# Encoder trunk on one core: the HGRN2 projections of eleven (head, sequence) pairs as plain products in place of seven products of quarters

## The chip, the cores and the metric

One Trainium2 chip; the kernel runs on one of its cores. The metric is the device time of one execution in microseconds (us), the median of the runs shown.

## The reference, cut to what matters

Two sequences of 16 meta tokens and 512 tokens (528 rows, 1024 features) pass through an MLA layer with its gated MLP and a bidirectional HGRN2 layer with its gated MLP, all in float32. The change lies in the HGRN2 layer, in `h @ w_in`:

```
def hgrn2_mixer(h, w_in, lb_param, o_norm, w_o, layer_idx):
    hp = jnp.pad(h, ((0, 0), (pad, 0), (0, 0)))
    proj = hp @ w_in                        # 1024 -> 5 * 1024
    q, i, f_fw, f_bw, g = jnp.split(proj, ...)
    ...
    o_fw = gla_chunked(qh, 1.0 - ff, vh, jnp.log(ff))
    o_bw = rev(gla_chunked(rev(qh), rev(1.0 - fb), rev(vh), rev(jnp.log(fb))))
    ...
    return o.astype(h.dtype) @ w_o
```

Eight heads of 128 columns each take q, f_fw, f_bw and g (four blocks of 1024 x 128 of `w_in`) and the values i.

## The kernel before

**Number format.** A float32 operand is held as two tiles in a rounded format, a high part h and a low part l = x - h. A product of two such operands is three matmuls, h*h, h*l and l*h, into one PSUM bank. A piece of weights is a [128, 1024] tile: eight blocks of 128 rows of one 128-column output block. Features lie as `act[s]`, [128, 8, 528] in h and in l for sequence s.

**Weights.** `Weights` walks a plan, piece by piece. `get` keeps one piece split and two raw pieces loaded ahead of the one in use: `_load` issues the DMA from HBM (`wraw`, 3 buffers), `split` casts the high half on ACT (L101) and subtracts the low half on POOL or DVE (L102), into `w` (3 buffers). `on_dve` names the pieces whose low half is DVE's; the pieces "p" of the HGRN2 projections are not among them, the value pieces "v" are. A piece that the second sequence needs again is stored split to HBM when its use starts (`kept_dr<-w`, 1 MB) and read back from there for s = 1 (`w<-kept_dr`).

**Units.** `hgrn` runs 16 units (h, s), the eight heads of sequence 0 and then of sequence 1. In each, TensorE computes `project(h, s)` into four tiles z0 to z3. In eight of them it also computes `values` for two heads (96 matmuls of 256 columns, for s = 0 also 24 for the meta tokens). After each yield of a projection, `step` advances the generators: `core` of the unit before last (scores, state, output) and `gates` of the last one (activations on ACT, scans and products on DVE). A scheduler then sets each engine's order; every engine works through its own queue in that order.

**Two kinds of projection.** In the units of `PLAIN`, (0,0), (1,0), (7,0), (0,1) and (7,1), each of the four blocks is 8 x 3 matmuls of 264 columns for each half of the tokens: 192 matmuls per unit, eight banks, evacuated in turn by ACT and DVE (L958). In the eleven others `seven` computes two blocks at a time as a 2 x 2 product of quarters with seven products in place of eight: 7 x 12 matmuls for each pair, 168 per unit, 14 banks. Its inputs are sums of quarters:

- of weights: `_mix` takes two raw pieces, forms four sums on POOL (L169 to L172), and splits them as seven 512-column parts in four pieces (ACT L109, low halves on DVE and POOL L110); the four pieces are stored for s = 1 (3.5 MB for each pair, 7 MB per unit, where four plain pieces are 4 MB);
- of features: `token_sums(s)` reads x back from HBM (`y<-x_dr`), forms four sums per step on DVE (L893 to L896), and splits them into the other sequence's tiles `act[1 - s]`, in the units of `SUMS_AT`, (1,0) for s = 0 and (0,1) for s = 1.

After the products come `e1` and `e5` (ACT copies, L990 and L998), five sums from PSUM on DVE and one on POOL (L1003) for each pair. Since sequence 1's tiles hold the sums of sequence 0, `load_x1` reads sequence 1's features back at unit (7,0), eight steps in one go.

```
h, s = f[1:]
finish()
if (h, s) == (HG - 1, 0):
    load_x1()
...
gens[:] = ([core(*units[n - 2])] if n > 1 else []) + [gates(*units[n - 1])]
if (h, s) in SUMS_AT:
    gens.append(token_sums(s))
for i, _ in enumerate(project(h, s)):
    if n > 1 or i >= SKIP:
        step()
```

Of the kernel before, what the change touches and what calls it, by code (L numbers as in the profile page):

```python
# [34 lines left out]
PLAIN = ((0, 0), (1, 0), (7, 0), (0, 1), (7, 1))  # L35
SUMS_AT = ((1, 0), (0, 1))
# [37 lines left out]
class Weights:  # L74
# [82 lines left out]
    def _mix(self, key, raws):  # L157

        nc = self.nc
        i, place = key[3], key[1] == "h"  # L160
        if i == 0:
            self.sums = raws
            return self.split(raws[0], 1024, nc.vector if place else nc.vector)
        if i == 1:
            v, g = self.sums
            a11, a12, a21, a22 = v[:, :512], v[:, 512:], g[:, :512], g[:, 512:]
            s1 = self.staging()[:, :512]
            s2, s3, s4 = (a11, a21, a12) if place else (self.staging()[:, :512] for _ in range(3))
            nc.gpsimd.tensor_tensor(s1, a21, a22, op=ALU.add)  # L169
            nc.gpsimd.tensor_tensor(s3, a11, a21, op=ALU.subtract)  # L170
            nc.gpsimd.tensor_tensor(s2, s1, a11, op=ALU.subtract)
            nc.gpsimd.tensor_tensor(s4, a12, s2, op=ALU.subtract)  # L172
            self.sums = (s2, s1), (s3, s4), (a22,)
        return self.split_parts(self.sums[i - 1], nc.gpsimd if i in ((2,) if place else (2,)) else nc.vector)
# [52 lines left out]
def mixed(h, s):  # L227

    return (h, s) not in PLAIN


def piece_place(key):

    kind = key[0]
    if kind == "mix":
        return ("mix", key[2][1], key[2][3], key[3]) if key[1] == "h" else None
    if kind == "p":
        return "p", key[1], key[3]
    if kind == "v":
        return ("v", key[1], key[3]) if len(key) == 4 else ("av", key[2])  # L240
    if kind == "in":
        return "in", key[2]
    if kind in ("rope", "pair"):
        return kind, *key[2:]
    if kind in ("wo", "up"):
        return kind, key[1], key[3]
    return None
# [8 lines left out]
def weight_plan(a):  # L256
# [51 lines left out]
    for f in hgrn_order():  # L308
        if f[0] == "v":
            for p in range(2):  # L310
                add(f + (p,), a["w_hgv"][2 * f[1] + p])
        elif mixed(*f[1:]):
            for p in range(2):
                add(("mix", "h", f + (p,), 0), a["w_hg"][f[1], 2 * p], a["w_hg"][f[1], 2 * p + 1])
                for i in range(1, 4):
                    add(("mix", "h", f + (p,), i))
        else:
            for i in range(4):
                add(f + (i,), a["w_hg"][f[1], i])
# [5 lines left out]
def tile_trunk(ctx: ExitStack, tc: tile.TileContext, a: dict, dbg=None):  # L325
# [532 lines left out]
    def hgrn(e_cm):  # L858
# [9 lines left out]
        W.staging = lambda: f1.tile([128, 512], F32, tag="s1", name="s1", bufs=1)  # L868

        def part(tag):  # L870
            return f1.tile([128, HT], F32, tag=tag, name=tag)

# [9 lines left out]
        def sums(s):  # L882

            return [t.rearrange("p k (c t) -> p (k c) t", c=2) for t in act[1 - s]]

        def token_sums(s):
            th, tl = sums(s)
            for k in range(4):
                y1, y2 = staged("y1"), staged("y2")
                nc.sync.dma_start(y1, x_dr[2 + s][:, k])  # L890
                nc.sync.dma_start(y2, x_dr[2 + s][:, 4 + k])
                b11, b12, b21, b22 = y1[:, :HT], y1[:, HT:], y2[:, :HT], y2[:, HT:]
                nc.vector.tensor_tensor(b11, b12, b11, op=ALU.subtract)  # L893
                nc.vector.tensor_tensor(b12, b22, b12, op=ALU.subtract)
                nc.vector.tensor_tensor(b22, b22, b11, op=ALU.subtract)
                nc.vector.tensor_tensor(b21, b21, b22, op=ALU.subtract)  # L896
                for i, y in enumerate((y1, y2)):
                    at = slice(8 * i + k, 8 * i + k + 5, 4)
                    split(th[:, at], tl[:, at], halves(y), nc.scalar, nc.gpsimd if i == 0 else nc.vector)
                yield  # L900

# [3 lines left out]
        def load_x1():  # L905
            for k in range(NK):
                r = staged()
                nc.sync.dma_start(r, x_dr[3][:, k])
                split(act[1][0][:, k], act[1][1][:, k], r, nc.scalar, nc.vector if k % 2 else nc.gpsimd)

# [35 lines left out]
        def project(h, s):  # L946
            z = [f1.tile([128, T], F32, tag=f"z{i}", name=f"z{i}", bufs=2) for i in range(4)]
            zs[h, s] = z
            if mixed(h, s):
                for p in range(2):  # L950
                    yield from seven(h, s, p, *z[2 * p : 2 * p + 2])
                return
# [7 lines left out]

        def seven(h, s, p, za, zb):

            th, tl = sums(s)
            xh, xl = act[s]

            def get(i):
                return W.get(("mix", "h", ("p", h, s, p), i))

            def product(w, w0, block):
                wh, wl = w  # L970
                ps = bank()[:, :HT]
                for k in range(4):
                    if isinstance(block, int):
                        j = 4 * (0, 3, 1, 2)[block] + k
                        bh, bl = th[:, j], tl[:, j]
                    else:
                        k0, c0 = block
                        bh, bl = xh[:, k0 + k, c0 : c0 + HT], xl[:, k0 + k, c0 : c0 + HT]
                    ws = slice(w0 + 128 * k, w0 + 128 * k + 128)
                    mm(ps, wh[:, ws], bh, start=k == 0, stop=False)  # L980
                    mm(ps, wh[:, ws], bl, start=False, stop=False)  # L981
                    mm(ps, wl[:, ws], bh, start=False, stop=k == 3)  # L982
                return ps

            tt = nc.vector.tensor_tensor
            lo, hi = slice(0, HT), slice(HT, T)
            e1, u2, u3, e5 = (part(n) for n in ("e1", "u2", "u3", "e5"))
            w = get(0)
            p1 = product(w, 0, (0, 0))
            nc.scalar.copy(e1, p1)  # L990
            p2 = product(w, 512, (4, 0))
            tt(za[:, lo], e1, p2, op=ALU.add)
            yield
            w = get(1)
            p6 = product(w, 0, 1)
            tt(u2, e1, p6, op=ALU.add)
            p5 = product(w, 512, 0)
            nc.scalar.copy(e5, p5)  # L998
            yield
            w = get(2)  # L1000
            p7 = product(w, 0, 2)
            tt(u3, u2, p7, op=ALU.add)
            nc.gpsimd.tensor_tensor(zb[:, hi], u3, e5, op=ALU.add)  # L1003
            tt(u2, u2, e5, op=ALU.add)
            p3 = product(w, 512, (4, HT))
            tt(za[:, hi], u2, p3, op=ALU.add)
            yield
            w = get(3)
            p4 = product(w, 0, 3)
            tt(zb[:, lo], u3, p4, op=ALU.add)  # L1010
            yield
# [237 lines left out]
        if order[0][1:] in SUMS_AT:  # L1249
            gens[:] = [token_sums(0)]  # L1250
# [25 lines left out]
        for f in order[1:]:  # L1276
# [6 lines left out]
            if (h, s) == (HG - 1, 0):  # L1283
                load_x1()
# [3 lines left out]
            if (h, s) in SUMS_AT:  # L1288
                gens.append(token_sums(s))
# [549 lines left out]
```

## Time and profile before

| | us |
|---|---|
| median of 3 runs | 3004.36 (3001.76 to 3009.07) |
| the profiled execution | 3010.18 |
| its span, first to last instruction | 3008.4 |
| of it the 16 units, first projection to last | 1475.4 to 2124.9 |

The mean granted TensorE clock of the profiled execution is 0.979. In a table by stretch, a busy time next to the length of the stretch tells how much of it the engine worked, and the count of matmuls tells what that work was; PEclk is the clock that was granted, 1.00 being 2.4 GHz and 0.50 being 1.2 GHz. Matmuls overlap: each is on record for some 0.28 us and the next one starts well before its end, so what a matmul costs is the distance from start to start. A wait names the instruction whose end released the waiting one.

### The profile page before, as it was taken

How to read it: one execution, taken by the hardware profiler on the slowest of the kernel's cores; microseconds unless marked ns; L12 is line 12 of the kernel's file. 1: busy time of each engine (PE TensorE's matmuls, PEld its weight loads, DVE VectorE, ACT ScalarE, POOL GpSimd, SP SyncE). 2: the span in 40 equal slices, each digit the busy share in tenths (PEclk: the TensorE clock that was granted, in tenths of full speed). 3: DMA queues.
4: the chain of work that ended last, by engine and by line, in shares of the span. 5: the costliest groups of instructions: out<-in, count | busy, mean ns of one | idle time of the engine just before them, and what ended most of it. 6: DMA issues, size and time to landing. Idle time of an engine off the chain costs nothing.

```text
span 3008.4 us, 54907 instructions
## 1 busy us (share of the span) xinstructions
PE 2846.8 (95%) x22138; PEld 2745.2 (91%) x22138; DVE 2152.8 (72%) x2872; ACT 1376.9 (46%) x2343; POOL 1436.0 (48%) x987
## 2 busy tenths in 40 slices
PE   8889999999899999999989899999999899999997
PEld 8888899899799999999978889999999899998886
DVE  5687777857988888443477877767659888886346
ACT  3355555544543444333254565445436444444343
POOL 5344444553677776443344442101315677774333
PEclk9999999999999999999999999999999999999999
DMA  7423222366322223554556675567666222225543
GB/s 257 154 95 114 93 88 85 123 219 244 146 82 81 69 86 94 188 174 125 162 184 256 240 261 191 202 247 258 230 246 225 75 74 77 86 77 188 168 151 116
DMA packets 151758, 468.50 MB, mean 156 GB/s; under 512 B 20576, under 2 KB 29792, under 8 KB 131280
## 3 DMA queue, kind: packets, MB, share of 16 engines
q1 hardware_dynamic: 147008, 455.33, 44.9%
q10 hardware_dynamic: 3168, 5.43, 0.6%
q8 instruction: 174, 2.85, 0.4%
q0 software_dynamic: 1328, 4.23, 0.4%
q14 instruction: 80, 0.66, 0.1%
HBM read 306.23 MB, written 154.30 MB: 153 GB/s over the span
## 4 chain that ended last, share of the span: by engine, by line
PE 34%; DVE 8%; ACT 3%; DMA 2%; issue 2%; POOL 1%; SPq 0%; DVEq 0%; ACTq 0%; POOLq 0%
PE mm L1565 4%; PE mm L1563 4%; PE mm L1564 4%; PE mm L1738 2%; PE mm L1739 2%; PE mm L1737 2%; PE mm L980 2%; PE mm L982 2%; PE mm L981 2%; PE mm L420 1%; PE mm L422 1%; PE mm L421 1%; PE a L1124 1%; PE mm L921 1%; DVE w L102 1%
## 5 line engine op out<-in xcount | busy, mean ns | idle before, releaser
L420 PE MATMUL mm<-ah,w 128*128 128x264 f32 x1824 | 534.0, 293 | 28.8 <-ACT w L101 9.5
L422 PE MATMUL mm<-ah,w 128*128 128x264 f32 x1824 | 526.5, 289 | 4.5 <-DVE w L102 2.3
L421 PE MATMUL mm<-al,w 128*128 128x264 f32 x1824 | 526.0, 288 | 2.8 <-DVE al L409 2.8
L101 ACT CAST w<-wraw 128x1024 fp32r<-128x1024 f32 (+3 forms) x254 | 234.2, 924 | 348.3 <-PE mm L1739 227.0
L420 PEld LDWEIGHTS mm<-ah,w 128*128 128x128 f32 x1824 | 351.0, 192 | 34.4 <-ACT w L101 9.5
L102 POOL TENSOR_TENSOR w<-wraw,w 128x1024 fp32r<-128x1024 f32 (+3 forms) x106 | 217.7, 2054 | 311.2 <-ACT w L101 280.7
L422 PEld LDWEIGHTS mm<-ah,w 128*128 128x128 f32 x1824 | 351.2, 193 | 4.9 <-DVE w L102 2.5
L421 PEld LDWEIGHTS mm<-al,w 128*128 128x128 f32 x1824 | 351.5, 193 | 4.3 <-DVE al L409 3.9
L1563 PE MATMUL mm<-ah,w 128*128 128x264 f32 x1216 | 347.8, 286 | 8.0 <-ACT w L101 6.6
L1565 PE MATMUL mm<-ah,w 128*128 128x264 f32 x1216 | 348.1, 286 | 6.7 <-DVE w L102 6.7
L1564 PE MATMUL mm<-al,w 128*128 128x264 f32 x1216 | 346.2, 285 | 0.0
L102 DVE TENSOR_TENSOR w<-wraw,w 128x1024 fp32r<-128x1024 f32 (+2 forms) x148 | 173.2, 1172 | 224.2 <-ACT w L101 220.3
L1738 PE MATMUL mm<-gl,w 128*128 128x264 f32 (+1 forms) x1012 | 324.1, 320 | 4.3 <-DVE gl L409 4.3
L1739 PE MATMUL mm<-gh,w 128*128 128x264 f32 (+1 forms) x1012 | 322.7, 319 | 2.9 <-DVE w L102 2.0
L1737 PE MATMUL mm<-gh,w 128*128 128x264 f32 (+1 forms) x1012 | 324.4, 321 | 0.5 <-DVE acc L1749 0.5
L1563 PE MATMUL mm<-th,w 128*128 128x264 f32 x912 | 259.9, 285 | 6.9 <-ACT e L1577 5.3
L1565 PE MATMUL mm<-th,w 128*128 128x264 f32 x912 | 260.4, 286 | 0.0
L1564 PE MATMUL mm<-tl,w 128*128 128x264 f32 x912 | 260.1, 285 | 0.0
L1563 PEld LDWEIGHTS mm<-ah,w 128*128 128x128 f32 x1216 | 230.6, 190 | 8.6 <-ACT w L101 7.1
L1565 PEld LDWEIGHTS mm<-ah,w 128*128 128x128 f32 x1216 | 230.6, 190 | 7.3 <-DVE w L102 7.3
L1564 PEld LDWEIGHTS mm<-al,w 128*128 128x128 f32 x1216 | 230.8, 190 | 0.0
L1738 PEld LDWEIGHTS mm<-gl,w 128*128 128x128 f32 x1012 | 191.9, 190 | 18.3 <-DVE gl L409 4.9
(365 smaller groups left out, 8463.6 us busy)
## 6 DMA issues: line engine op xcount, KB each, us to landing
kept_dr<-w SPq DMA_DIRECT2D x79, 1024.0 KB, 6.6
w<-kept_dr SPq DMA_DIRECT2D x79, 1024.0 KB, 6.2
wraw<-w_up SPq DMA_DIRECT2D x88, 512.0 KB, 4.0
wraw<-w_dn SPq DMA_DIRECT2D x88, 384.0 KB, 3.3
g_dr<-c SPq DMA_DIRECT2D x38, 528.0 KB, 2.7
wraw<-w_hg SPq DMA_DIRECT2D x36, 512.0 KB, 4.7
wraw<-w_dn SPq DMA_DIRECT2D x25, 512.0 KB, 3.6
x_dr<-acc SPq DMA_DIRECT2D x48, 264.0 KB, 2.4
```

The source lines that it names most:

```text
L101: self.nc.scalar.copy(h[:, :n], src)
L102: engine.tensor_tensor(l[:, :n], src, h[:, :n].bitcast(F32), op=ALU.subtract)
L420: mm(out, wh[:, ws], xh[:, x0 + k, cs], start=first and i == 0, stop=False)
L421: mm(out, wh[:, ws], xl[:, x0 + k, cs], start=False, stop=False)
L422: mm(out, wl[:, ws], xh[:, x0 + k, cs], start=False, stop=last and i == n - 1)
L980: mm(ps, wh[:, ws], bh, start=k == 0, stop=False)
L1563: mm(out, wh[:, ws], bh, start=k == 0, stop=False)
L1564: mm(out, wh[:, ws], bl, start=False, stop=False)
L1565: mm(out, wl[:, ws], bh, start=False, stop=k == 3)
L1737: mm(o, wh[:, ws], gh[:, cs], start=k == 0, stop=False)
L1738: mm(o, wh[:, ws], gl[:, cs], start=False, stop=False)
L1739: mm(o, wl[:, ws], gh[:, cs], start=False, stop=k == NJ - 1)
```

## The change

`PLAIN`, `mixed`, `seven`, `token_sums` and the HGRN2 part of `_mix` go. All 16 units project by 192 matmuls from four plain pieces, with the low halves on POOL. The features of sequence 1 are read back by `load_x1`, now a generator that does one of its eight steps at a time, attached at unit (4,0) (`REREAD`). The MLP stages keep their sums of quarters.

```
-PLAIN = ((0, 0), (1, 0), (7, 0), (0, 1), (7, 1))
-SUMS_AT = ((1, 0), (0, 1))
+REREAD = (4, 0)
...
-        elif mixed(*f[1:]):
-            for p in range(2):
-                add(("mix", "h", f + (p,), 0), a["w_hg"][f[1], 2 * p], a["w_hg"][f[1], 2 * p + 1])
-                for i in range(1, 4):
-                    add(("mix", "h", f + (p,), i))
         else:
             for i in range(4):
                 add(f + (i,), a["w_hg"][f[1], i])
...
             z = [f1.tile([128, T], F32, tag=f"z{i}", name=f"z{i}", bufs=2) for i in range(4)]
             zs[h, s] = z
-            if mixed(h, s):
-                for p in range(2):
-                    yield from seven(h, s, p, *z[2 * p : 2 * p + 2])
-                return
             for i in range(4):
...
         order = hgrn_order()
-        if order[0][1:] in SUMS_AT:
-            gens[:] = [token_sums(0)]
...
-            if (h, s) == (HG - 1, 0):
-                load_x1()
             if (h, s) == (HG - 1, 1):
                 load_o(1, 0, range(HG), staged)
             gens[:] = ([core(*units[n - 2])] if n > 1 else []) + [gates(*units[n - 1])]
-            if (h, s) in SUMS_AT:
-                gens.append(token_sums(s))
+            if (h, s) == REREAD:
+                gens.append(load_x1())
```

**DVE, end of unit (1,0) and start of (2,0).** `y` are the rows of features of which sums are formed, `b` the gates' scan, `vm` the values of the meta tokens, `al` the low half of sequence 1's features. Before:

```order
L1035 SCALAR_TENSOR_TENSOR b_17677<-ends,b_17677 128x528
L893 TENSOR_TENSOR y_17277<-y_17277 128x264
L1048 TENSOR_TENSOR b_17673<-b_17673,bm_17823 128x512
L894 TENSOR_TENSOR y_17277<-y_17278,y_17277 128x264
L1048 TENSOR_TENSOR b_17677<-b_17677,bm_17856 128x512
L895 TENSOR_TENSOR y_17278<-y_17278,y_17277 128x264
```

After:

```order
L942 SCALAR_TENSOR_TENSOR b_17624<-ends,b_17624 128x528
L955 TENSOR_TENSOR b_17620<-b_17620,bm_17756 128x512
L955 TENSOR_TENSOR b_17624<-b_17624,bm_17797 128x512
L903 TENSOR_TENSOR vm<-vm,mm_17544 16x256 x2
L396 TENSOR_TENSOR al_16765<-xr,ah_16764 128x528
```

The sums `y` are gone from between the scan and the products `b`. The re-read of sequence 1's features stands here already, two units ahead of where the code attaches it.

**ACT, start of unit (3,0).** `v` is the last evacuation of the values, `e` and `z` evacuations of the projection, `w` the casts of high halves. Before:

```order
L924 COPY v<-mm_18140 128x256
L1046 COPY bm_18403<-b_18253 128x8
L379 ACTIVATE head<-bm_18403 128x8
L1046 COPY bm_18436<-b_18257 128x8
L379 ACTIVATE head<-bm_18436 128x8
L109 CAST w<-wraw 128x512
L109 CAST w<-s_18197 128x512
L939 COPY vm<-mm_18166 16x256
L109 CAST w<-wraw 128x512 x2
L990 COPY e_18193<-mm_18208 128x264
L939 COPY vm<-mm_18166 16x256
```

After:

```order
L887 COPY v<-mm_18064 128x256
L953 COPY bm_18302<-b_18166 128x8
L953 COPY bm_18343<-b_18170 128x8
L366 ACTIVATE head<-bm_18302 128x8
L366 ACTIVATE head<-bm_18343 128x8
L100 CAST w<-wraw 128x1024
L902 COPY vm<-mm_18090 16x256
L100 CAST w<-wraw 128x1024
L902 COPY vm<-mm_18090 16x256
L917 COPY z_18113<-mm_18123 128x264
L1019 COPY kT_18151<-a 128x384
```

Four casts of 512 columns, one of them of a POOL sum, gave way to two of 1024. The first evacuation stands at the same place, but of a bank that 24 matmuls fill in place of 12.

**POOL, the units (2,0) and (3,0).** `s` and `wraw` are the sums of quarters, `atm` belongs to the core. Before:

```order
L169 TENSOR_TENSOR s_17872<-wraw 128x512
L409 TENSOR_TENSOR al_16765<-y_17330,ah_16764 128x2x264
L1144 TENSOR_TENSOR atm<-amm_17114,amm_17115 16x16
L170 TENSOR_TENSOR wraw<-wraw 128x512
L1003 TENSOR_TENSOR z_17610<-u_17615,e_17616 128x264
L171 TENSOR_TENSOR wraw<-s_17872,wraw 128x512
L172 TENSOR_TENSOR wraw<-wraw 128x512
L110 TENSOR_TENSOR w<-wraw,w 128x512 x2
```

After:

```order
L101 TENSOR_TENSOR w<-wraw,w 128x1024 x2
L396 TENSOR_TENSOR al_16765<-xr,ah_16764 128x528
L101 TENSOR_TENSOR w<-wraw,w 128x1024 x2
L1051 TENSOR_TENSOR atm<-amm_17114,amm_17115 16x16
L396 TENSOR_TENSOR al_16765<-xr,ah_16764 128x528 x2
L101 TENSOR_TENSOR w<-wraw,w 128x1024
```

The sums and their halves gave way to the low halves of whole pieces, with the low halves of four of sequence 1's feature rows between them.

## Rows read from the trace of the kernel before

**Rows 1.** The page's first part: the span, and the busy time, share and instructions of TensorE, its weight loads and the other engines.

```profile
span 3008.4 us, 54907 instructions
PE 2846.8 (95%) x22138; PEld 2745.2 (91%) x22138; DVE 2152.8 (72%) x2872; ACT 1376.9 (46%) x2343; POOL 1436.0 (48%) x987
```

**Rows 2.** Busy time of each engine by stretch, one stretch a unit, from the first matmul of its projection to that of the next. In order: (1,0), (2,0), (3,0), (4,0), (5,0), (6,0), (7,0), (0,1), (1,1), then (3,1), (4,1) and (7,1). Columns: the stretch, its length, busy us and instructions of PE, PEld, DVE, ACT, POOL, the granted clock, the DMA engines' busy share, GB/s.

```profile
1505.90:1549.00 43.10, 38.64 (x306) 38.23 (x305) 34.68 (x52) 31.54 (x57) 21.15 (x16) 0.96 0.59 198
1549.00:1610.50 61.50, 48.92 (x389) 46.51 (x388) 45.67 (x76) 29.38 (x57) 25.30 (x19) 0.89 0.61 223
1610.50:1648.40 37.90, 33.02 (x276) 30.77 (x274) 31.31 (x59) 16.31 (x40) 17.17 (x14) 0.95 0.68 246
1648.40:1702.50 54.10, 48.57 (x400) 46.36 (x401) 42.20 (x71) 35.61 (x67) 23.31 (x19) 0.94 0.69 249
1702.50:1737.70 35.20, 30.80 (x264) 28.49 (x262) 31.67 (x57) 15.37 (x36) 17.11 (x13) 1.00 0.68 251
1737.70:1791.70 54.00, 48.58 (x413) 46.02 (x414) 43.42 (x74) 37.29 (x71) 25.27 (x16) 0.97 0.70 249
1791.70:1826.30 34.60, 31.58 (x274) 30.51 (x272) 23.37 (x49) 13.78 (x32) 13.36 (x8) 1.00 0.87 314
1826.30:1872.20 45.90, 45.90 (x394) 44.90 (x395) 33.38 (x70) 30.45 (x59) 11.06 (x9) 0.97 0.43 146
1872.20:1906.30 34.10, 31.20 (x275) 29.26 (x274) 30.51 (x55) 14.15 (x36) 15.20 (x11) 1.00 0.31 105
...
1948.80:1978.70 29.90, 29.90 (x276) 29.09 (x275) 18.59 (x47) 7.09 (x23) 2.48 (x3) 1.00 0.71 249
1978.70:2020.40 41.70, 41.70 (x373) 40.87 (x372) 28.14 (x62) 26.76 (x53) 3.05 (x3) 1.00 0.66 239
...
2092.20:2124.90 32.70, 32.70 (x299) 31.99 (x298) 19.04 (x42) 11.72 (x30) 7.95 (x5) 1.00 0.64 218
```

**Rows 3.** TensorE in order of time in unit (1,0): the start of each matmul, its time on record, line and shape. 78 matmuls of 264 columns stand from the first row to the second, 14 of 256 columns from the third to the fourth, 9 from the fifth to the sixth.

```profile
1519.75 0.28 PE L420 MATMUL mm<-ah,w 128*128 128x264 f32 x1
...
1529.14 0.29 PE L422 MATMUL mm<-ah,w 128*128 128x264 f32 x1
...
1536.15 0.42 PE L921 MATMUL mm<-w,ah 128*128 128x256 f32 x1
...
1538.93 0.41 PE L922 MATMUL mm<-w,al 128*128 128x256 f32 x1
...
1539.33 0.28 PE L921 MATMUL mm<-w,ah 128*128 128x256 f32 x1
...
1540.26 0.28 PE L923 MATMUL mm<-w,ah 128*128 128x256 f32 x1
```

**Rows 4.** What TensorE waited for (us in total, times, longest): the first four rows in the units (2,0) to (6,0), the next two in (1,0), the next in (7,0), the last two in (1,1) to (7,1).

```profile
PE mm L980 <- ACT e L990: 15.4, 5, 8.8
PE mm L982 <- DVE w L110: 12.7, 9, 3.5
PE mm L981 <- DVE al L409: 1.3, 1, 1.3
PE mm L980 <- ACT sq L434: 1.2, 1, 1.2
...
PE mm L923 <- DVE w L102: 2.9, 1, 2.9
PE mm L921 <- ACT w L101: 1.6, 1, 1.6
...
PE mm L420 <- ACT z L958: 3.0, 1, 3.0
...
PE mm L982 <- DVE w L102: 1.1, 1, 1.1
PE mm L980 <- ACT e L990: 1.1, 1, 1.1
```

**Rows 5.** DVE and then ACT in order of time at the start of unit (2,0), with the idle time ahead of an instruction and what ended it in brackets.

```profile
1554.82 0.43 DVE L893 TENSOR_TENSOR y<-y 128x264 f32<-128x264 f32 x1 [5.26 <-DMA y<-x_dr]
...
1556.23 0.63 ACT L406 CAST ah<-y 128x528 fp32r<-128x528 f32 x1 [5.55 <-DVE y L894]
...
1561.34 0.38 ACT L990 COPY e<-mm 128x264 f32<-128x264 f32 x1
```

**Rows 6.** Unit (7,0), a plain unit that splits its weights itself: ACT (two rows), then POOL; the last row is POOL in unit (1,0).

```profile
1803.15 0.63 ACT L406 CAST ah<-xr 128x528 fp32r<-128x528 f32 x1 [3.09 <-DMA xr<-x_dr]
...
1824.39 0.63 ACT L406 CAST ah<-y 128x528 fp32r<-128x528 f32 x1 [7.27 <-DVE y L894]
...
1793.98 4.75 POOL L102 TENSOR_TENSOR w<-wraw,w 128x1024 fp32r<-128x1024 f32 x2 [7.43 <-ACT w L101]
...
1540.75 7.69 POOL L171 TENSOR_TENSOR wraw<-s,wraw 128x512 f32<-128x512 f32 x1 [8.55 <-DVE dt L1078]
```

**Rows 7.** Groups of instructions by line in the stretch 1560 to 2180 us (busy us, mean ns of one, idle time ahead and its releaser): the high and the low half of a whole piece.

```profile
L101 ACT CAST w<-wraw 128x1024 fp32r<-128x1024 f32 x29 | 30.3, 1044 | 23.7 <-issue 10.1 <-PE mm L982 2.8 <-DVE z L1006 2.7
...
L102 POOL TENSOR_TENSOR w<-wraw,w 128x1024 fp32r<-128x1024 f32 x12 | 30.1, 2508 | 51.3 <-ACT w L101 51.3
```

More of the change, by code (lines that the diff above doesn't have):

```diff
@@ L159, in _mix @@
         nc = self.nc
-        i, place = key[3], key[1] == "h"
+        i = key[3]
         if i == 0:
             self.sums = raws
-            return self.split(raws[0], 1024, nc.vector if place else nc.vector)
+            return self.split(raws[0], 1024, nc.vector)
         if i == 1:
@@ L167, in _mix @@
             s1 = self.staging()[:, :512]
-            s2, s3, s4 = (a11, a21, a12) if place else (self.staging()[:, :512] for _ in range(3))
+            s2, s3, s4 = (self.staging()[:, :512] for _ in range(3))
             nc.gpsimd.tensor_tensor(s1, a21, a22, op=ALU.add)
@@ L173, in _mix @@
             self.sums = (s2, s1), (s3, s4), (a22,)
-        return self.split_parts(self.sums[i - 1], nc.gpsimd if i in ((2,) if place else (2,)) else nc.vector)
+        return self.split_parts(self.sums[i - 1], nc.gpsimd if i == 2 else nc.vector)
     def get(self, key):
@@ L224, in hgrn_order @@
     return out
-def mixed(h, s):
-    return (h, s) not in PLAIN
 def piece_place(key):
     kind = key[0]
-    if kind == "mix":
-        return ("mix", key[2][1], key[2][3], key[3]) if key[1] == "h" else None
     if kind == "p":
@@ L867, in hgrn @@
         xm = f1.tile([128, NK, 128], F32R, name="xm")
-        W.staging = lambda: f1.tile([128, 512], F32, tag="s1", name="s1", bufs=1)
-        def part(tag):
-            return f1.tile([128, HT], F32, tag=tag, name=tag)
         def meta_cols():
@@ L880, in meta_cols @@
                 split(h, l, raw[:, s], nc.scalar, nc.vector)
[L882 to L900, printed above, removed]
         def staged(name="xr"):
@@ L909, in load_x1 @@
                 split(act[1][0][:, k], act[1][1][:, k], r, nc.scalar, nc.vector if k % 2 else nc.gpsimd)
+                yield
         def values(hp, s):
@@ L959, in project @@
                     yield
[L961 to L1011, printed above, removed]
         def gates(h, s):
```

## The prediction

> **What bounds the kernel now.** I read the page's first part, then busy times unit by unit, then the spacing of matmuls, then TensorE's waits and the queues behind the longest of them. TensorE has most work, 95% of the span [rows 1], and in most of the program no other engine sets the pace. The table by unit shows where that fails. In (3,1), (4,1) and (7,1) PE is busy for the whole stretch: 29.9, 41.7 and 32.7 us [rows 2]. In (2,0) to (6,0) it isn't, and the lengths differ though the matmuls are the same: (3,0) has 276 in 37.9 us, (3,1) has 276 in 29.9 us. What differs is who makes the weights. For s = 1 they arrive split from HBM; for s = 0 sums and halves are formed on the spot, and DVE works 31.3 us in (3,0) and 18.6 in (3,1), ACT 16.3 and 7.1, POOL 17.2 and 2.5 [rows 2].
>
> To size the loss I need the cost of a matmul from start to start. 264 columns: (1529.14 - 1519.75) / 77 = 0.122 us. 256 columns: (1540.26 - 1539.33) / 8 = 0.116 us, and, where the granted clock was 1.2 GHz, (1538.93 - 1536.15) / 13 = 0.214 us [rows 3]. The other matmuls of a unit (cores, column sums) follow from (3,1): 29.9 - 168 x 0.122 = 9.4 us for 108, 0.087 each. Check on (7,1), all plain: 192 x 0.122 + 107 x 0.087 = 32.7 us, as measured [rows 2].
>
> Time without loss, then, against the stretch [rows 2]:
> - (2,0) to (7,0), 277.3 us, 2016 matmuls: 5 x 168 + 192 = 1032 of projections (125.9), 3 x 120 of values (41.8), 624 others (54.3), together 222.0. Lost: 55.3.
> - (1,0), 43.1 us: 192 x 0.122 + 114 x 0.116 = 36.6. Lost: 6.5.
> - (0,1), 45.9 us: 23.4 + 96 x 0.116 + 106 x 0.087 = 43.7. Lost: 2.2.
> - (1,1), 34.1 us: 20.5 + 107 x 0.087 = 29.8. Lost: 4.3.
>
> Sum 68.3 us. It has three parts. Waits on record come to 40.3 us, nearly all on weights just split or on ACT's evacuation of `e` [rows 4]. The clock fell in six of these units after such waits: a granted clock of 0.96, 0.89, 0.95, 0.94, 0.97 and 0.97 is 33 us at 1.2 GHz [rows 2], and by 0.116 against 0.214 us each costs 46%, 15 us. The rest, 13 us, is restart after a wait.
>
> **The change, part by part.**
>
> Added matmuls: eleven units go from 168 to 192, 264 more, 264 x 0.122 = **+32.2 us**, all on TensorE's path; nothing hides them. Between (3,1) and (7,1) the same step reads 2.8 us for 23 on record [rows 2].
>
> Feature sums removed. DVE idled 5.26 us at `y` until its DMA landed, ACT behind it 5.55 us at the cast of a sum, the copy of `e` came at 1561.34, and TensorE waited 8.8 us for it [rows 4, 5]. For (0,1)'s sums ACT idled 7.27 us in (7,0) [rows 6] and TensorE 3.0 [rows 4]. Both causes go. What is next behind them is the gates' work, which (3,1) and (4,1) carry without a wait.
>
> Weight sums, recombination and extra halves removed. The difference between (3,0) and (3,1) is their price per unit without values: 12.7 us of DVE, 9.2 of ACT, 14.7 of POOL [rows 2]. Plain pieces put back 4 casts of 1.04 us on ACT and 4 halves of 2.5 us on POOL [rows 7], and nothing on DVE but four evacuations that take the place of sums. So DVE and ACT come near to their load in (7,1), 19.0 and 11.7 us of 32.7, and the 12.7 us of waits for DVE's halves [rows 4] have no instruction left to end them.
>
> Lookahead. A plain piece feeds 48 matmuls, 5.86 us, while the next is split in 1.04 + 2.5 = 3.5 us; a part of 512 columns fed 12, 1.5 us. An evacuation now frees a bank that takes 2.9 us to fill, before 1.5: with three banks ACT may be late by twice as much. That is why the order on ACT in front of (3,0), hardly shorter than before, should cost TensorE less. (7,0) is the row for it: it splits its own four pieces, and no wait there is for a weight [rows 4].
>
> Stores and loads. 4 MB per unit in place of 7; DMA is busy 61 to 70% in (2,0) to (6,0) [rows 2] and ends almost no wait [rows 4], so I take nothing for it.
>
> The re-read moves from (7,0) to the units (2,0) and (3,0), where the order puts its casts and halves. Eight transfers, casts and halves are the same as before. SP takes them between the weight loads; ACT can wait at a cast for a transfer, as it did for 3.09 us in (7,0) [rows 6], with evacuations queued behind it. Bounds: nothing, to 3 us once per pair of buffers, 12 us. I take 3.
>
> What stays. (7,0) lost 34.6 - 192 x 0.122 - 82 x 0.087 = 4.1 us, 3.0 of it the wait above: 1.1 us for a plain unit that splits its own weights; for (1,0) to (7,0) 7.7 us. The value pieces made TensorE wait 4.5 us in (1,0), and not in the other three units with values of s = 0 [rows 4]; the feature sums stood on the engines it waited for, and I keep half, 2.3. With the re-read, 13 us; the bounds are 0 and the 38 us of the first rival.
>
> Sum: 32.2 - 68.3 + 13 = **-23 us**. The profiled execution took 3010.18 us (span 3008.4), 5.8 above the median of the runs; the change is small beside both, so I subtract from the median: 3004.4 - 23 = **2981 us**.
>
> **The rivals.**
>
> *All of it comes back.* 32.2 - 68.3 = -36: 2968 us. For it: (7,1) and (3,1) lose nothing. Against: units of s = 0 still cast and halve.
>
> *ACT stays late.* ACT's queue in front of a projection still holds gates, casts and copies in one line. Waits that ACT ended are 15.4 + 1.2 + 1.6 + 3.0 + 1.1 = 22.3 of the 40.3 us [rows 4]; if that share of the loss stays, 38 us, the change comes to 32.2 - 68.3 + 38 = +2: 3006 us. Against: the longest of them hung on `y`, and banks last twice as long.
>
> *POOL sets the pace (slower).* All 20 new pieces of (2,0) to (6,0) have their low half on POOL, none on DVE. One POOL instruction took 7.69 us on record while DVE ran on without a break [rows 6]. If halves stretched so, 1.04 + 7.69 = 8.7 us stand against the 5.86 us of a piece, 2.9 us of wait for each, 57 in all: 32.2 - 68.3 + 57 = +21: 3025 us. It decides from a half of 5.86 - 1.04 = 4.8 us on. Against: the two halves of whole pieces in (7,0) took 4.75 us together [rows 6], and the mean of twelve is 2.5 [rows 7]. The Trainium skill, SBUF — State Buffer, on who interferes with whom, says that a DVE instruction with two SBUF inputs and a GpSimd instruction that reads SBUF exclude each other, whichever starts first; by that rule a half of two SBUF inputs could wait out one DVE instruction at its start, and the trace shows halves of 2.5 us beside a busy DVE.
>
> *Nothing comes back (slower).* If the lost time belongs to the gates and cores and not to sums, the busiest engine just gets 32 us more: 3037 us. Against: (3,0) and (3,1) have the same gates and cores. The Trainium skill, Perfetto Trace Analysis, on identifying the most-contended engine, says to take the engine of highest occupancy as the one to relieve first; by TensorE's 95% that speaks against adding matmuls, but the table by unit has it short of work in just these units.
>
> **How the numbers follow.** Forecast (-14 to -32) 0.62; all of it 0.12; ACT late 0.14; POOL 0.07; nothing back 0.05. About 0.3%, 9 us, is what a measurement of this kernel can tell from no change. Faster by more than that: the first two, and the lower fifth of ACT late, 0.77. Within it: most of ACT late, 0.11. Slower: POOL, nothing back, 0.12. A range of 2966 to 3004 holds the forecast, most of the first rival and half of ACT late, some 0.8.
>
> **What would show it.** Units (3,0) and (5,0) at 32 to 34 us; (2,0), (4,0) and (6,0) at 47 to 50; (1,1) to (6,1) about 2.9 us longer each, save (1,1), which stays near 33; no wait of TensorE over 3 us between (1,0) and (7,1), and a granted clock of 1.00 in most units. Wrong, if TensorE waits at each piece for POOL's half (the POOL rival), at evacuations for ACT (ACT late), or if casts of the re-read hold ACT for more than 3 us.

## The result and the profile after

| | before | after |
|---|---|---|
| median of the runs beside each other, us | 3003.06 (2998.86 to 3009.07, 4 runs) | 2973.95 (2972.63 to 2976.31, 4 runs) |
| the profiled execution, us | 3010.18 | 2974.06 |
| its span, us | 3008.4 | 2972.3 |

The ratio is 0.9897, with an interval of 0.9885 to 0.9909: 29 us faster. The profiled executions differ by 36 us, since that of before lay 7 us above its median.

The page's first part, against [rows 1]:

```profile
span 2972.3 us, 54808 instructions
PE 2849.2 (96%) x22402; PEld 2757.8 (93%) x22402; DVE 2027.9 (68%) x2696; ACT 1342.9 (45%) x2275; POOL 1336.4 (45%) x905
```

264 matmuls more, and TensorE's busy time is only 2.4 us higher. Busy time holds matmuls that go slowly at 1.2 GHz too (0.214 us each in [rows 3] in place of 0.116), and there are fewer of these.

The table by unit, against [rows 2], in the same order: (1,0) to (7,0), (0,1), (1,1), then (3,1), (4,1), (7,1).

```profile
1503.60:1540.30 36.70, 36.70 (x307) 36.70 (x306) 27.53 (x41) 28.73 (x51) 10.47 (x12) 1.00 0.80 277
1540.30:1588.20 47.90, 46.38 (x413) 45.41 (x411) 27.68 (x53) 26.09 (x54) 15.84 (x9) 1.00 0.72 254
1588.20:1621.00 32.80, 32.80 (x298) 32.07 (x299) 19.96 (x43) 14.10 (x33) 13.21 (x6) 1.00 0.70 240
1621.00:1667.50 46.50, 46.50 (x413) 45.70 (x412) 29.96 (x56) 31.55 (x60) 8.85 (x4) 1.00 0.60 195
1667.50:1700.20 32.70, 32.70 (x300) 31.97 (x299) 17.07 (x41) 12.17 (x27) 12.48 (x6) 1.00 0.67 240
1700.20:1746.70 46.50, 46.50 (x413) 45.70 (x412) 29.97 (x57) 31.54 (x60) 8.85 (x4) 1.00 0.56 184
1746.70:1779.40 32.70, 32.70 (x300) 31.97 (x299) 17.62 (x42) 11.28 (x27) 9.04 (x5) 1.00 0.58 210
1779.40:1824.40 45.00, 44.59 (x396) 43.75 (x395) 26.79 (x56) 28.79 (x57) 4.28 (x3) 1.00 0.46 160
1824.40:1857.20 32.80, 32.80 (x301) 32.07 (x299) 15.08 (x39) 7.86 (x24) 1.86 (x2) 1.00 0.46 161
...
1901.70:1934.40 32.70, 32.70 (x299) 31.99 (x298) 15.07 (x39) 7.12 (x23) 0.53 (x1) 1.00 0.45 161
1934.40:1979.00 44.60, 44.60 (x397) 43.78 (x396) 24.86 (x54) 26.93 (x53) 1.04 (x1) 1.00 0.39 139
...
2056.30:2089.00 32.70, 32.70 (x300) 31.97 (x299) 17.29 (x40) 10.36 (x27) 6.61 (x4) 1.00 0.58 200
```

PE's busy time is now the length of the stretch nearly everywhere, and the granted clock is 1.00 in every unit from (1,0) to (7,1). A plain unit without values takes 32.7 to 32.8 us whether it splits its weights itself or reads them split; (3,0) fell from 37.9 us with 276 matmuls on record to 32.8 with 298. The longer s = 1 units, (3,1) from 29.9 to 32.7 and (4,1) from 41.7 to 44.6 us, are the price. DVE in (3,0) fell from 31.3 to 20.0 us and POOL from 17.2 to 13.2, with the re-read of sequence 1's features among it.

All of TensorE's waits from (1,0) to (7,1), against [rows 4]:

```profile
PE mm L407 <- ACT v L887: 1.5, 1, 1.5
PE o L1036 <- DVE r L1094: 0.4, 1, 0.4
```

From the first projection of (0,0) to the end of (7,1) the units took 649.5 us before and 615.9 after, 33.6 less. The 40 us of waits are 1.9 us.

### The profile page after: what moved, and what is told of

Read it like the earlier page. It is cut to its first block, busy times and chain, and to the rows that moved or that the text cites. A ratio compares the mean times of both kernels' runs of the same rounds, so it can differ in the third digit from the quotient of the medians.

```text
span 2972.3 us, 54808 instructions
## 1 busy us (share of the span) xinstructions
PE 2849.2 (96%) x22402; PEld 2757.8 (93%) x22402; DVE 2027.9 (68%) x2696; ACT 1342.9 (45%) x2275; POOL 1336.4 (45%) x905
## 4 chain that ended last, share of the span: by engine, by line
PE 39%; DVE 5%; issue 2%; ACT 2%; DMA 2%; POOL 1%; SPq 0%; DVEq 0%; ACTq 0%; POOLq 0%
PE mm L407 4%; PE mm L409 4%; PE mm L1468 4%; PE mm L1466 4%; PE mm L408 4%; PE mm L1467 4%; PE mm L1641 2%; PE mm L1642 2%; PE mm L1640 2%; PE a L1058 1%; PE mm L885 1%; PE a L1031 1%; PE mm L884 1%; PE mm L886 1%; DMA xr<-x_dr 1%
## 5 line engine op out<-in xcount | busy, mean ns | idle before, releaser
L407 PE MATMUL mm<-ah,w 128*128 128x264 f32 x2528 | 737.8, 292 | 27.2 <-ACT w L100 10.0
L409 PE MATMUL mm<-ah,w 128*128 128x264 f32 x2528 | 725.7, 287 | 4.5 <-DVE w L101 2.3
L408 PE MATMUL mm<-al,w 128*128 128x264 f32 x2528 | 724.2, 286 | 2.7 <-DVE al L396 2.7
L407 PEld LDWEIGHTS mm<-ah,w 128*128 128x128 f32 x2528 | 482.2, 191 | 34.2 <-ACT w L100 10.0
L409 PEld LDWEIGHTS mm<-ah,w 128*128 128x128 f32 x2528 | 482.3, 191 | 4.9 <-DVE w L101 2.5
L408 PEld LDWEIGHTS mm<-al,w 128*128 128x128 f32 x2528 | 482.6, 191 | 4.4 <-DVE al L396 3.8
L101 POOL TENSOR_TENSOR w<-wraw,w 128x1024 fp32r<-128x1024 f32 (+3 forms) x126 | 267.1, 2122 | 429.9 <-ACT w L100 398.7
L100 ACT CAST w<-wraw 128x1024 fp32r<-128x1024 f32 (+3 forms) x262 | 242.6, 928 | 342.6 <-PE mm L1642 221.3
L1466 PE MATMUL mm<-ah,w 128*128 128x264 f32 x1216 | 347.1, 285 | 8.0 <-ACT w L100 6.7
L1468 PE MATMUL mm<-ah,w 128*128 128x264 f32 x1216 | 347.6, 286 | 6.9 <-DVE w L101 6.9
L1467 PE MATMUL mm<-al,w 128*128 128x264 f32 x1216 | 345.7, 284 | 0.0
L101 DVE TENSOR_TENSOR w<-wraw,w 128x1024 fp32r<-128x1024 f32 (+2 forms) x136 | 158.4, 1166 | 215.6 <-ACT w L100 215.1
L1466 PEld LDWEIGHTS mm<-ah,w 128*128 128x128 f32 x1216 | 229.9, 189 | 8.6 <-ACT w L100 7.1
L1468 PEld LDWEIGHTS mm<-ah,w 128*128 128x128 f32 x1216 | 230.0, 189 | 7.4 <-DVE w L101 7.4
L1467 PEld LDWEIGHTS mm<-al,w 128*128 128x128 f32 x1216 | 230.1, 189 | 0.0
L1642 PEld LDWEIGHTS mm<-gh,w 128*128 128x128 f32 x1012 | 191.2, 189 | 17.9 <-DVE w L101 2.2
```

What stands on the lines that cost most here:

```text
L100: self.nc.scalar.copy(h[:, :n], src)
L101: engine.tensor_tensor(l[:, :n], src, h[:, :n].bitcast(F32), op=ALU.subtract)
L407: mm(out, wh[:, ws], xh[:, x0 + k, cs], start=first and i == 0, stop=False)
L408: mm(out, wh[:, ws], xl[:, x0 + k, cs], start=False, stop=False)
L409: mm(out, wl[:, ws], xh[:, x0 + k, cs], start=False, stop=last and i == n - 1)
L1466: mm(out, wh[:, ws], bh, start=k == 0, stop=False)
```

## The experiments

The changed kernel measured 2973.95 us, the kernel before some 3003 us beside every group of runs. Where an expectation names a number for the changed kernel, it is compared with that median.

**How much do the 264 matmuls cost?**

```
-                    linear([ps] * 2, wh, wl, act[s], range(NK), c_range=(c,))
+                    ks = range(NK if h in (0, 7) or (h, s) == (1, 0) else NK - 1)
+                    linear([ps] * 2, wh, wl, act[s], ks, c_range=(c,))
```

> The changed kernel, but in the eleven units that had seven products one of the eight blocks of the contraction is left out (7 of 8, so 168 matmuls in place of 192); the values are not the reference's. It sizes the added matmuls without any sums. Theory (the changed kernel is bound by TensorE in every unit): 264 x 0.122 = 32 us less than the changed kernel, 2942 us. Rival (another engine or the stores stand just behind TensorE): half of it or less, 2958 us or more.

Measured: 2942.56 us (ratio to before 0.9799, 0.9784 to 0.9813), 31.4 us less than the changed kernel. The added matmuls cost what the spacing of [rows 3] says, and within these 31 us nothing stands behind TensorE. It also sizes the loss of the kernel before: with as many matmuls and no sums it could have taken 2943 us, so 60 us were lost.

**Which sums made the loss?** First without the sums of features (the read-back kept, at (1,0)):

```
-SUMS_AT = ((1, 0), (0, 1))
+SUMS_AT = ((1, 0),)
...
-            if (h, s) == (HG - 1, 0):
-                load_x1()
...
-                gens.append(token_sums(s))
+                gens.append(load_x1())
```

> The kernel before with its seven products, but without the sums of features: the products take sequence 1's features as they are, read back step by step at unit (1,0) (no re-read at (7,0)), and for sequence 1 those of sequence 0. So the four DVE sums per step are left out, and the products' values are not the reference's. Theory (two causes, features and weights, each with its own waits): the 8.8 us wait in (2,0), the 4.5 us in (1,0) and the 3.0 us in (7,0) go with their restart and clock, some 20 us: 2983 us. Rival (weight sums alone make the waits, the feature sums only stood nearby): within 6 us of before, 2997 us or more.

Measured: 2993.95 us (0.9972, 0.9961 to 0.9982), 9 us less. Between the two expectations: the wait of 8.8 us went, and (2,0) became 9.1 us shorter, but waits for DVE's weight halves stayed, 10.9 us in nine, the longest 3.4 us. In (1,0) most of the 4.5 us [rows 4] stayed too:

```profile
PE mm L924 <- DVE w L102: 2.5, 1, 2.5
PE mm L922 <- ACT w L101: 0.4, 1, 0.4
```

This run reads sequence 1's features back in (1,0), and that unit takes 44.3 us, 1.2 more than before. So the 9 us are the price of the feature sums less that of the read-back in this place.

Then without the sums of weights:

```
+            if place:
+                self.sums = (a11, a21), (a12, a22), (a22,)
+                return self.split_parts(self.sums[0], nc.vector)
```

> The kernel before, but the raw quarters of the weights are split as they are in place of their sums: the four POOL sums per pair of blocks are left out in the HGRN2 units, all casts, halves, stores, recombination and matmuls stay; the values are not the reference's. Theory (weights made on the spot are late because POOL sums stand ahead of casts and halves): the waits for DVE's halves (12.7 us) and part of ACT's go, some 25 to 30 us: 2975 us. Rival (pieces of 1.5 us of matmuls and banks of 12 matmuls are too short a lookahead, with or without sums): 8 us or less: 2995 us.

Measured: 2970.17 us (0.9893, 0.9876 to 0.9910), 33 us less: as fast as the changed kernel, with 264 matmuls fewer and all of the recombination. The four POOL instructions per pair were the larger part of the loss. How they lengthened it shows in the groups by line from 1549 to 1830 us, about (2,0) to (7,0): ACT's casts of parts, DVE's halves (of the parts that stand in raw pieces, then of the sum in the staging tile `s`) and POOL's third sum (busy us, mean ns | idle time ahead), first in the kernel before:

```profile
L109 ACT CAST w<-wraw 128x512 fp32r<-128x512 f32 x40 | 23.8, 616 | 16.3 <-POOL wraw L171 13.7 <-POOL wraw L172 2.4 <-DMA kept_dr<-w 0.2
...
L110 DVE TENSOR_TENSOR w<-wraw,w 128x512 fp32r<-128x512 f32 x20 | 20.6, 1028 | 4.4 <-ACT w L109 4.4
...
L110 DVE TENSOR_TENSOR w<-s,w 128x512 fp32r<-128x512 f32 x10 | 10.5, 1054 | 0.4 <-ACT w L109 0.4
...
L171 POOL TENSOR_TENSOR wraw<-s,wraw 128x512 f32<-128x512 f32 x9 | 12.7, 1412 | 19.6 <-DVE w L102 13.4 <-issue 6.2
```

and without the weight sums:

```profile
L110 DVE TENSOR_TENSOR w<-wraw,w 128x512 fp32r<-128x512 f32 x30 | 22.6, 772 | 0.0
```

The chain has three links. POOL waited for DVE's half of the first piece (its third sum overwrites that raw piece). ACT idled 13.7 us at casts until that sum was done: all four casts in front of (3,0) are of POOL sums, three of which stand in raw pieces. And DVE's halves got longer, 772 ns in the mean without the sums and 1028 and 1054 with them. The long ones did not stand beside a sum, though, but beside POOL's own halves. Of the 30 halves before, 17 took 0.66 to 0.69 us; 11 took over 1.1 us, all of them beside a half of POOL's and only two beside a sum as well. One of these and one of DVE's alone, then the two halves of POOL's that stand beside the first:

```profile
1583.74 1.75 DVE L110 TENSOR_TENSOR w<-wraw,w 128x512 fp32r<-128x512 f32 x1
1590.10 0.68 DVE L110 TENSOR_TENSOR w<-wraw,w 128x512 fp32r<-128x512 f32 x1
...
1583.21 3.41 POOL L110 TENSOR_TENSOR w<-wraw,w 128x512 fp32r<-128x512 f32 x2
```

Without the weight sums two of the halves took over 1.1 us, again beside POOL's. That the sums brought both engines' halves to the same moment fits this; no run shows it by itself. The Trainium skill, SBUF — State Buffer, on who interferes with whom, has a DVE instruction with two SBUF inputs and a GpSimd instruction that reads SBUF exclude each other; 0.68 us alone and some 1.75 beside a half of POOL's agree with it.

Both left out together (the two edits above):

> Seven products with neither kind of sum: the POOL sums of weights and the DVE sums of features of the kernel before are left out (raw quarters and plain features in their place), all else stays; the values are not the reference's. Theory (the two causes are separate, so their shares of 33 and 9 us add): 2960 us, which leaves 18 us over the 2942 us that 168 matmuls take on the changed kernel's path, for halves of small pieces and recombination. Rival (both lengthen the same waits): 2968 us, hardly below the run without weight sums. Third (sums were all that was late): 2945 us.

Measured: 2963.36 us (0.9866, 0.9851 to 0.9881), 39 us less than before. The shares of 33 and 9 us nearly add; the two expectations of 2960 and 2968 us are not told apart. Some 21 us over the 2943 us remain, and of the lost 60 us they belong to neither kind of sum: DVE's halves of small parts still ended 6.4 us of waits, ACT's evacuations 4.5. The table by unit says where they lie. First (3,0) and (3,1) here, then the same two with 168 plain matmuls:

```profile
1591.90:1623.70 31.80, 31.01 (x280) 29.60 (x278) 26.28 (x58) 16.20 (x38) 8.08 (x7) 1.00 0.77 290
1899.00:1928.80 29.80, 29.80 (x275) 29.05 (x274) 18.56 (x47) 7.03 (x23) 2.47 (x3) 1.00 0.72 249
...
1586.40:1616.60 30.20, 29.87 (x275) 29.09 (x274) 20.58 (x42) 12.89 (x32) 16.27 (x7) 1.00 0.70 248
1882.90:1912.70 29.80, 29.80 (x275) 29.08 (x274) 15.05 (x39) 7.12 (x23) 0.53 (x1) 1.00 0.49 183
```

(3,1) has the whole recombination, but reads its parts split, and takes 29.8 us in both. So recombination by itself costs nothing there. The six units whose small parts are split on the spot, (2,0) to (6,0) and (1,1), are 17.5 us longer here in all, of which (2,0), next to the read-back, has 5.1.

**Could the sums have come earlier?** Raw pieces for the seven products loaded four plan entries ahead, with two more buffers:

```
+            if key[:2] == ("mix", "h") and not raws:
+                r = self.more.tile([128, 1024], F32, tag="wraw", name="wraw", bufs=2)
...
-            while self.nd < min(self.ns + 2, last):
+            while self.nd < min(self.ns + self.ahead(), last):
```

> The kernel before with two more buffers for raw weights in the HGRN2 layer and raw pieces of the seven products loaded four plan entries ahead in place of two; nothing left out (e5 shares a tile with e1). Theory (the POOL sums came late because their raw pieces landed late: POOL idled 57 us in front of the first sum until a load landed): some 25 us less than before, 2978 us. Rival (the chain of four sums, cast and half is itself too long for pieces of 2.9 us of matmuls): within 8 us of before, 2995 us or more.

Measured: 2986.16 us (0.9937, 0.9920 to 0.9953), 17 us less: between the two. POOL's idle time shows what its sums waited for, first the kernel before, the groups of the third and the first sum in all units:

```profile
L171 POOL TENSOR_TENSOR wraw<-s,wraw 128x512 f32<-128x512 f32 x12 | 23.0, 1915 | 33.4 <-DVE w L102 18.7 <-DVE dt L1078 8.6 <-issue 6.2
...
L169 POOL TENSOR_TENSOR s<-wraw 128x512 f32<-128x512 f32 x12 | 16.5, 1378 | 57.5 <-DMA wraw<-w_hg 57.5
```

and with early loads, the first and the third:

```profile
L172 POOL TENSOR_TENSOR s<-wraw 128x512 f32<-128x512 f32 x12 | 18.6, 1548 | 19.5 <-DVE w L110 10.5 <-DMA wraw<-w_hg 9.0
...
L174 POOL TENSOR_TENSOR wraw<-s,wraw 128x512 f32<-128x512 f32 x12 | 16.5, 1376 | 43.7 <-DVE w L102 43.7
```

57.5 us of waiting for loads became 9.0, and the sum that overwrites the first raw piece now waits 43.7 us for DVE's half of it, 18.7 before. Part of the wait moved one link down its chain. Idle time of POOL is not yet time of TensorE; of TensorE's own waits, those for DVE's halves fell little (12.9 us before, from (1,0) to (7,1)), those for ACT's `e` by more than half (16.5 before):

```profile
PE mm L990 <- DVE w L110: 9.9, 9, 2.4
PE mm L988 <- ACT e L998: 6.4, 5, 1.6
```

**Do the sums cost by themselves, with plain products?** The features' sums back, with all units plain (sums used by nothing):

```
-PLAIN = ((0, 0), (1, 0), (7, 0), (0, 1), (7, 1))
+PLAIN = tuple((h, s) for s in range(2) for h in range(8))
```

> All units project by plain products, but the sums of features are still formed (at (1,0) and (0,1), used by nothing) and sequence 1's features are read back at (7,0) as before. Theory (they cost by themselves): the waits in (2,0), (1,0) and (7,0) come back in part, with banks that last twice as long: 6 to 16 us over the changed kernel, 2985 us. Rival (only together with seven products): 2974 us, the changed kernel's.

Measured: 2983.95 us (0.9936, 0.9919 to 0.9953), 10 us over the changed kernel, which is the theory's size. By unit, (1,0), (2,0) and (3,0):

```profile
1506.80:1547.50 40.70, 37.37 (x306) 36.74 (x304) 31.27 (x49) 29.38 (x55) 13.91 (x14) 1.00 0.73 249
1547.50:1601.20 53.70, 49.26 (x411) 48.27 (x412) 39.52 (x65) 31.04 (x61) 19.63 (x11) 0.94 0.73 257
1601.20:1633.90 32.70, 32.70 (x300) 31.97 (x299) 25.93 (x47) 13.14 (x30) 15.09 (x7) 1.00 0.76 265
```

(1,0) is 4.0 and (2,0) 5.8 us longer than in the changed kernel, and (3,0) the same. So the sums cost by themselves. In (1,0) and then (2,0) TensorE waited for

```profile
PE mm L921 <- ACT v L924: 1.5, 1, 1.5
...
PE a L1124 <- ACT kT L1114: 4.4, 1, 4.4
PE mm L420 <- ACT v L924: 1.6, 1, 1.6
```

The 4.4 us are the mechanism of before: the copy of `kT` (the transposed keys of a core) stood on ACT behind a cast of a sum, at which ACT had waited 2.92 us for DVE's `y`. But the waits for value pieces in (1,0), 4.5 us before [rows 4], are not among them, and most of them stayed without the feature sums, with the read-back in their place; what made them stays open. Nor did the wait in (7,0) come back: that unit, with the re-read in one go, takes 32.7 us.

POOL's sums back, as additions of zeros ahead of each cast in (2,0) to (6,0):

```
+            if key[0] == "p" and key[2] == 0 and 2 <= key[1] <= 6:
+                for c in range(2):
+                    x = raws[0][:, 512 * c : 512 * c + 512]
+                    self.nc.gpsimd.tensor_tensor(x, x, self.zeros, op=ALU.add)
```

> The changed kernel, but each plain piece of the units (2,0) to (6,0) passes two additions of zeros on POOL, in place and of 512 columns each, ahead of its cast: the load of the weight sums and their place in the chain, without seven products; the result is the same. Theory (a long piece hides it nearly: 2 x 1.4 + 1.04 + 2.5 = 6.3 us against 5.86 us of matmuls, 0.5 us of wait for 20 pieces): 10 us over the changed kernel, 2984 us. Rival (lookahead hides it whole): 2974 us. Second rival (POOL's work slows DVE, so that it comes late everywhere): 2994 us or more.

Measured: 2989.59 us (0.9952, 0.9937 to 0.9967), 16 us more, between the theory and its second rival, and the theory's mechanism was wrong: nothing is lost piece by piece. By unit, (2,0), (3,0) and (6,0):

```profile
1547.20:1600.50 53.30, 48.41 (x411) 46.85 (x411) 36.84 (x57) 26.75 (x54) 32.26 (x19) 0.97 0.67 231
1600.50:1633.40 32.90, 32.90 (x299) 32.17 (x299) 27.69 (x43) 14.16 (x33) 21.64 (x14) 1.00 0.58 203
1713.20:1764.80 51.60, 49.50 (x412) 48.56 (x411) 33.00 (x56) 31.70 (x60) 14.16 (x7) 0.93 0.61 215
```

(3,0), POOL busy 21.6 of 32.9 us and DVE 27.7, loses 0.1 us; (2,0) loses 5.4 and (6,0) 5.1. (1,0), at whose end the first pieces of (2,0) are made, loses 3.0 us, (4,0) 0.6. So the loss sits in units with values. TensorE waited there for ACT's evacuations of values, at the start of and in (2,0); for the core's result `r`, in (6,0); for DVE's half of a value piece, in (1,0); and for DVE's evacuation of the projection:

```profile
PE mm L411 <- ACT v L893: 3.4, 2, 3.1
PE o L1042 <- DVE r L1100: 2.4, 2, 2.1
PE mm L892 <- DVE w L101: 2.2, 1, 2.2
PE mm L419 <- DVE z L923: 2.1, 2, 1.7
```

**Do longer banks hide ACT's delay?** Two banks in place of three:

```
-    def bank(tag="mm1", bufs=3):
+    def bank(tag="mm1", bufs=2):
```

> The changed kernel with two PSUM banks in place of three for projections, values and column sums. Theory (engines are seldom late now, so a bank of 24 matmuls is slack enough): 0 to 6 us over the changed kernel, 2977 us. Rival (slack of the banks is what took the waits of ACT away): 15 us or more over it, 2989 us or more.

Measured: 2984.65 us (0.9936, 0.9921 to 0.9950), 11 us more: neither expectation. Its waits were two kinds only, in (1,0) to (7,1):

```profile
PE mm L407 <- DVE vm L903: 2.4, 1, 2.4
PE mm L407 <- DVE z L917: 1.4, 2, 0.9
```

The waits on record are 3.8 us, 1.4 of them in (1,0) and 2.4 in (3,0). (1,0) takes 38.6 and (3,0) 35.8 us, 1.9 and 3.0 more than with three banks, and (3,1), which has no wait, 33.1 in place of 32.7. The third bank is worth something even where no wait is on record, but by these rows ACT was not what it had to cover.

**Is there a faster version?** What the runs suggested: sequence 0 plain, sequence 1 with seven products, its summed pieces made during sequence 0 from raw pieces that are there anyway, beside TensorE's path.

```
+SIDE = (3, 5)
...
-    return (h, s) not in PLAIN
+    return s == 1 and h in SIDE
...
+            if key[0] == "p" and key[2] == 0 and key[1] in SIDE:
+                if key[3] % 2:
+                    self.jobs.append(self.quarters(key[1], key[3] // 2, self.first, raws[0]))
+                else:
+                    self.first = raws[0]
...
+                nc.scalar.copy(t[:, 0], src)
+                nc.vector.tensor_tensor(t[:, 1], src, t[:, 0].bitcast(F32), op=ALU.subtract)
+                nc.sync.dma_start(self.kept[at][:, :, 512 * c : 512 * c + 512], t.bitcast(F32))
```

> A version after the findings: sequence 0 projects plainly, as in the changed kernel; sequence 1 takes seven products for heads 3 and 5 alone. Its pieces of summed weights are made during sequence 0 from the raw pieces that are there anyway, beside TensorE's path (four POOL sums, casts on ACT, halves on DVE, stored to HBM); only sequence 1's feature sums are needed, at (0,1). Theory (sums cost only where TensorE waits for them): 2 x 24 x 0.122 = 5.9 us less matmul, some 1.5 us back at (0,1) as before: 2970 us. Rival (the work itself disturbs the units of sequence 0, wherever it is put): 2980 us or more.

> The same with heads 2 to 6 (120 matmuls less, 14.6 us), which leaves unit (1,0), where the layer before still ends, alone. Theory: 2974 - 14.6 + 1.5 + 4 = 2965 us; below the version with six heads if unit (1,0) is the tight one. Rival: 2980 us or more.

> The same with heads 1 to 6, so that 144 matmuls go. Theory: 17.6 us less matmul, 1.5 us back at (0,1), and some 5 us in the units of sequence 0 with values, where POOL sums ahead of whole pieces cost 3 to 5 us a unit: 2963 us. Rival (the work disturbs the units of sequence 0): 2980 us or more.

Measured: 2978.78 us for two heads (0.9920, 0.9905 to 0.9935), 3001.00 for five (0.9992, 0.9982 to 1.0001), 3024.70 for six (1.0069, 1.0053 to 1.0086). None beats the changed kernel, and six heads are slower than before: the rival holds for five and six heads, and for two the time lies just under it, 9 us over the theory. Sequence 1 gained as forecast; in the version with six heads (3,1) is 29.9 us again. Sequence 0 lost more. Units (4,0), with 74 matmuls more on record than in the changed kernel, and (6,0) with six heads, then (3,1):

```profile
1642.60:1705.60 63.00, 57.21 (x487) 54.69 (x488) 49.42 (x84) 38.63 (x73) 23.12 (x15) 0.92 0.65 236
...
1746.20:1818.40 72.20, 57.08 (x418) 54.38 (x417) 44.20 (x72) 38.99 (x72) 27.31 (x17) 0.81 0.57 205
1971.20:2001.10 29.90, 29.90 (x277) 29.12 (x275) 18.56 (x47) 7.12 (x23) 2.47 (x3) 1.00 0.70 250
```

and what TensorE waited for most in sequence 0:

```profile
PE mm L456 <- POOL w L104: 10.4, 6, 2.5
PE mm L454 <- ACT w L103: 8.6, 3, 3.9
```

Work that nobody waits for at once still stands in the same queues: POOL's sums stand ahead of the low half of the next whole piece, and with six heads POOL's half is what TensorE waits for most. The mechanism of the prediction's POOL rival acts in this kernel, but doesn't decide it: 10.4 us are less than a quarter of its waits in sequence 0, with five heads it is 3.7 us, and with two none.

**The one wait that was left.** The scheduler had put the re-read into (2,0) and (3,0); this version holds its casts back to (4,0):

```
-                split(act[1][0][:, k], act[1][1][:, k], r, nc.scalar, nc.vector if k % 2 else nc.gpsimd)
+                with tc.issue_after(Table.users[-1]):
+                    split(act[1][0][:, k], act[1][1][:, k], r, nc.scalar, nc.vector if k % 2 else nc.gpsimd)
```

> The changed kernel with the casts of the re-read held back on ACT until the instructions of unit (4,0), where the code attaches it; in the changed kernel the scheduler put them two units earlier, and a cast that waited 4.28 us for its transfer in (2,0) ended in TensorE's only wait over 1 us of the units, 1.5 us. Theory (that wait was the place, not the work): unit (2,0) loses its 1.5 us and (4,0) gains none, 2972 us, hardly to be told from the changed kernel's 2974 by the time, but by the waits. Rival (eight casts in one unit queue ACT behind transfers as in (7,0) of the kernel before): waits of 3 us and more in (4,0), 2977 us or more.

Measured: 2974.86 us (0.9908, 0.9891 to 0.9925): by the time no different from the changed kernel. By the trace the theory holds: in the changed kernel ACT, in order of time,

```profile
1578.88 0.64 ACT L393 CAST ah<-xr 128x528 fp32r<-128x528 f32 x1 [4.28 <-DMA xr<-x_dr]
...
1587.75 0.37 ACT L887 COPY v<-mm 128x256 f32<-128x256 f32 x1
```

and with the casts held back, TensorE's only wait on record from (1,0) to (7,1):

```profile
PE o L1037 <- DVE r L1095: 0.3, 1, 0.3
```

(2,0) takes 46.2 us in place of 47.9, and (4,0) 46.4.

## Why the prediction was right

The direction, the place and the range held; 2981 us were forecast and 2974 measured, -29 us in place of -23. One term was much too large, and an error the other way hid part of it (4).

1. *Added matmuls, +32.2 us.* Right: 31.4 us when taken out again.
2. *Lost time of 68.3 us.* Right in size and place. The units became 33.6 us shorter, so 32.2 + 33.6 = 65.8 us came back in the profiled executions, in the units named. In the medians it is 31.4 + 29.1 = 60.5 us, because the profiled execution of before was slower than its median.
3. *The causes.* Both held: feature sums 9 us (less what the read-back in (1,0) cost that run), weight sums 33 us in the kernel before, 39 together. Some 21 us of the loss belong to neither; they lie mostly where small parts are split on the spot, which the prediction named in one breath with sums and recombination. How the weight sums' 33 us divide between their place in the chain and the load on DVE and POOL stays open: earlier loads alone gave 17 back, which is place; DVE halves of 1.75 us beside POOL's halves are load.
4. *What stays, 13 us: this term was mis-sized.* 1.9 us of waits stayed. Its parts: 1.1 us for each plain unit of s = 0, taken from (7,0), measured 0.0 to 0.1 (32.7 and 32.8 us, the same as for s = 1), so (7,0)'s remainder was no price of splitting, and likely restart after its wait; 2.3 us for value pieces in (1,0), measured 0, but not for the reason given, that half of those waits hung on the feature sums: without these sums, but with the read-back in (1,0), 2.9 of the 4.5 us stayed, and with them and plain products none came back; 3 us for the re-read, measured 1.5 us, with the mechanism named: a cast that waited for its transfer, and an evacuation behind it. Without this term the sum is -36 us, and the profiled executions differ by 36; that rival, 2968 us, is as near to the median as the forecast. That the forecast came within 7 us is in part luck: the loss by the rows, 68.3 us, is 7.8 more than the 60.5 of the medians, most of it because the execution that gave the rows was slower than its median, and this offset most of the 11 us by which the term was too large.
5. *The lookahead of pieces and banks.* The longer piece was shown: with POOL's sums ahead of each cast, (3,0) loses 0.1 us. The longer bank was not: with two banks TensorE waits for DVE, not for ACT.
6. *The rivals.* ACT late: no. POOL sets the pace: no in this change; with sums put beside the path its halves were the largest of several waits (10.4 us in six). Nothing comes back: no, and the kernel before without POOL's sums, at 2970 us, shows that gates and cores were not the limit.
7. *What would show it.* (3,0) and (5,0) 32.8 and 32.7 us (32 to 34 forecast); (2,0), (4,0), (6,0) 47.9, 46.5 and 46.5 (47 to 50, so two a little below); (1,1) 32.8 (near 33); (3,1) and (4,1) 2.8 and 2.9 longer, (2,1) and (6,1) 2.0 and 2.4. No wait of TensorE over 3 us; clock 1.00. One sign of being wrong did show: a cast of the re-read held ACT for 4.28 us, over the 3 us named, and cost TensorE only 1.5 us.

## What to carry to other kernels

A scheme that saves an eighth of the busiest engine's matmuls is worth what that engine can keep of it: here 264 fewer saved 31 us and lost 60, some 39 of them by the sums that make the inputs, and most of the rest where small parts are split on the spot. Look at busy time stage by stage before the share of the whole span, and price a saving by the stage in which the saved engine waits. Moving the preparing work off the path doesn't make it free while it stands in the same in-order queues.

## What was not expected of the hardware

A unit that splits its own weights and one that reads them split take the same time to 0.1 us, at DMA shares from 0.45 to 0.70. And with two PSUM banks, a unit without any wait on record still took 33.1 us in place of 32.7; by what, the trace doesn't show.
